# Weighted sum over experts on one core: VectorE's loop over single rounds, ScalarE copying the sums out

## The chip, the cores and the metric

The kernel runs on one core of a Trainium2 chip. The metric is the device time of one launch in microseconds (us). The kernel before took 704.42 us, the median of three runs (704.29 to 704.84).

## The reference

`expert_outputs` has the shape 16 x 1024 x 8 x 512 and `combine_weights` 16 x 1024 x 8, both float32. For each of the 16384 tokens the eight expert rows of 512 numbers are weighted and added:

```python
weights = combine_weights[..., np.newaxis]
return np.sum(expert_outputs * weights, axis=2).astype(np.float32)
```

268 MB are read and 33.6 MB written; each number read is used once.

## The kernel before

The 16384 tokens are 128 token rows of 128 partitions each, here called tiles; a tile is 128 x 8 x 512 numbers, 2 MB. The first 120 tiles are worked in 12 rounds of 10 tiles, the last 8 tiles are the tail.

One buffer, `ring`, holds the ten input tiles of a round. SyncE loads it in three chunks of 4, 4 and 2 tiles (L138); a chunk of the next round is loaded as soon as VectorE has finished the tiles of this round that stood there (the semaphore `done` counts finished tiles). The eight tail tiles are loaded the same way (L146), as one piece of three tiles and five of one.

VectorE does nearly all the arithmetic. For each chunk one instruction writes the product of expert 0 into `acc` (L227), and 14 instructions for each pair of tiles add the other seven experts (L217: `acc = ring * weight + acc`). `acc` holds 20 tiles, two halves of ten, and the loop body is two rounds (h = 0 and 1), run six times. The weights of a round are read from `w_c`, which ScalarE fills from `w_t` by one small copy a round (L173), after the store of two rounds before has landed, since that copy is also VectorE's leave to overwrite that half of `acc`.

ScalarE issues the stores of rounds 0 to 10 (L104), SyncE that of round 11. Round 8 (`SHARED`) is shared: ScalarE stores the middle half of each partition's row and GpSimd the two ends (L119, L122), with two tiny loads into `spare` around it (L127).

In the tail TensorE works as well. ScalarE scales an identity matrix by a column of weights (`diag`, L180, four buffers), and TensorE multiplies it with a tile's expert rows into PSUM (L193), 32 products in all, in the order of the tiles; a product needs its `diag` and its loaded tile. VectorE adds the remaining experts to what stands in PSUM (L217, L255), and one last addition (L269) closes tile 7. SyncE stores tiles 0 to 5 and then tiles 6 and 7 (L150).

All engines run in program order; what comes later in an engine's queue waits behind an instruction that waits.

Of the kernel before, what the change touches and what calls it, by code (L numbers as in the profile page):

```python
# [10 lines left out]
def kernel(  # L11
# [9 lines left out]

    nc = tc.nc
    fp32 = mybir.dt.float32
    mult, add = mybir.AluOpType.mult, mybir.AluOpType.add

    B, S, E, D = expert_outputs.shape
    T = B * S
    P = 128
    R = 10  # L40
    G = 2 * R
    T_P = T // P
    GROUPS = T_P // G
    LOOP = GROUPS * G
    TAIL = T_P - LOOP
    ROUNDS = LOOP // R
    CHUNKS = [(0, 4), (4, 4), (8, 2)]
    C = len(CHUNKS)
    DIAGS = 4
    OURS = 120  # L50
    END = 5 * D // 2
    APART = R * D - END
    SHARED = ROUNDS - 4

    x = expert_outputs.rearrange("b s e d -> (b s) e d")
    w = combine_weights.rearrange("b s e -> (b s) e")
    o = out.rearrange("b s d -> (b s) d")
    cut = LOOP * P
    x_g = x[0:cut].rearrange("(p n b g) e d -> n b p g e d", p=P, b=2, g=G)
    w_g = w[0:cut].rearrange("(p t) e -> p t e", p=P)  # L60
    o_g = o[0:cut].rearrange("(p n b g) d -> n b p g d", p=P, b=2, g=G)
    x_t = x[cut:T].rearrange("(p j) e d -> p j e d", j=TAIL)
    w_x = w[cut:T].rearrange("(p j) e -> p j e", j=TAIL)
    o_t = o[cut:T].rearrange("(p j) d -> p j d", j=TAIL)


    pe_e = [4, 4, 3, 3, 4, 5, 5, 4]
    tail_loads = [(0, 3)] + [(j, 1) for j in range(3, TAIL)]
# [4 lines left out]
    one = ctx.enter_context(tc.tile_pool(name="one", bufs=1))  # L73
    psum = ctx.enter_context(tc.tile_pool(name="psum", bufs=1, space=bass.MemoryType.PSUM))
    ring = one.tile([P, R, E, D], fp32, name="ring")
    acc = one.tile([P, G, D], fp32, name="acc")
    w_t = one.tile([P, T_P, E], fp32, name="w_t")
    w_c = one.tile([P, G, E], fp32, name="w_c")
    spare = one.tile([16, 8], fp32, name="spare")
    ident = one.tile([P, P], fp32, name="ident")  # L80
    diag = one.tile([P, DIAGS, P], fp32, name="diag")
    ps = psum.tile([P, TAIL, D], fp32, name="ps")

    sem = tc.alloc_semaphore
    w_in = sem("w_in")
    w_set = [sem(f"w_set{h}") for h in range(2)]
    loaded = [sem(f"loaded{c}") for c in range(C)]
    stored = [sem(f"stored{h}") for h in range(2)]
    rest_out = sem("rest_out")
    step = sem("step")  # L90
    done = sem("done")
    tail_in = [sem(f"tail_in{k}") for k in range(len(tail_loads))]
# [3 lines left out]
    product = sem("product")  # L96

    def store(queue, n):
        h = n % 2
        queue.wait_ge(done, (n + 1) * R)  # L100
        out = o_g[n // 4, n // 2 % 2].rearrange("p g d -> p (g d)")
        first, last = (END, APART) if n == SHARED else (h * R * D, (h + 1) * R * D)
        sums = acc.rearrange("p g d -> p (g d)")[:, first:last]
        queue.dma_start(out=out[:, first:last], in_=sums).then_inc(stored[h], 16)  # L104

    def ends(n, first, last):

        assert n % 2 == 0
        return [
            a.rearrange("p g d -> p (g d)")[:, 0 : 2 * APART]  # L110
            .rearrange("p (b k) -> p b k", b=2)[:, :, first:last]
            for a in (o_g[n // 4, n // 2 % 2], acc)
        ]

    def store_ends(gpsimd):
        turn(gpsimd, 4, 0)
        gpsimd.wait_ge(done, (SHARED + 1) * R)
        o_r, a_r = ends(SHARED, 0, END)
        gpsimd.dma_start(out=o_r[0:OURS], in_=a_r[0:OURS]).then_inc(rest_out, 16)  # L119
        for k in range(2):  # L120
            o_r, a_r = ends(SHARED, k * END // 2, (k + 1) * END // 2)
            gpsimd.dma_start(out=o_r[OURS:P], in_=a_r[OURS:P]).then_inc(rest_out, 16)  # L122
        turn(gpsimd, 13, 4)

    def turn(gpsimd, k, b):

        gpsimd.dma_start(  # L127
            out=spare[0:k, b : b + 4].rearrange("p (i j) -> p i j", i=2)[:, :, 0:1],
            in_=w[0 : 2 * k].rearrange("(p i) e -> p i e", i=2)[:, :, 0:1],
        ).then_inc(rest_out, 16)  # L130

    def loads_and_last_stores(sync):
        for n in range(ROUNDS):
            for c, (r, m) in enumerate(CHUNKS):
                if n:
                    sync.wait_ge(done, (n - 1) * R + r + m)
                g = n % 2 * R + r
                sync.dma_start(  # L138
                    out=ring[:, r : r + m], in_=x_g[n // 4, n // 2 % 2, :, g : g + m]
                ).then_inc(loaded[c], 16)  # L140
                if n == 0 and c == 0:
                    sync.dma_start(out=w_t[:, 0:LOOP], in_=w_g).then_inc(w_in, 16)
                    sync.dma_start(out=w_t[:, LOOP:T_P], in_=w_x).then_inc(w_in, 16)
        for k, (j, m) in enumerate(tail_loads):
            sync.wait_ge(done, LOOP - R + j + m)
            sync.dma_start(out=ring[:, j : j + m], in_=x_t[:, j : j + m]).then_inc(tail_in[k], 16)  # L146
        store(sync, ROUNDS - 1)
        for j, m in tail_stores:
            sync.wait_ge(done, LOOP + j + m)
            sync.dma_start(out=o_t[:, j : j + m], in_=acc[:, j : j + m]).then_inc(tail_out, 16)  # L150
# [12 lines left out]

    def weights_and_stores(scalar):
        scalar.wait_ge(w_in, 32)
        for n in range(ROUNDS):
            h = n % 2
            if n >= 2:
                store(scalar, n - 2)
                scalar.wait_ge(stored[h], 16 * (n // 2))  # L170
            if n == SHARED + 2:
                scalar.wait_ge(rest_out, 16 * 5)
            scalar.copy(  # L173
                out=w_c[:, h * R : h * R + R], in_=w_t[:, n * R : n * R + R]
            ).then_inc(w_set[h], 1)
        store(scalar, ROUNDS - 2)
        scalar.wait_ge(id_set, 2)
        scalar.wait_ge(stored[0], 16 * ROUNDS // 2)
        for k, (j, e) in enumerate(diags):
            i = scalar.mul(out=diag[:, k % DIAGS], in_=ident, mul=w_t[:, LOOP + j, e : e + 1])  # L180
            i.then_inc(diag_set, 1)
            if k >= DIAGS:
                i.wait_op(product, k - DIAGS + 1, "sem-ge")
        scalar.wait_ge(stored[1], 16 * ROUNDS // 2)

    def first_terms(tensor):
        for k, (j, e) in enumerate(diags):
# [13 lines left out]
    def terms(vector):  # L201
        def take(s, v):
            vector.wait_ge(s, v).then_inc(s, -v)  # L203

        last = {}

        def count(i, g, e):

            if e == E - 1:
                i.then_inc(done, 1)  # L210
            else:
                i.then_inc(step, 1)
                last["all"] = last.get("all", 0) + 1
                last[g] = last["all"]

        def fused(g, e, weight, before):
            return vector.scalar_tensor_tensor(  # L217
                out=acc[:, g], in0=ring[:, g % R, e], scalar=weight, in1=before, op0=mult, op1=add
            )

        with nc.Fori(0, GROUPS, engines=OrderedEngineSet([vector.engine])):
            for h in range(2):
                take(w_set[h], 1)
                for c, (r, m) in enumerate(CHUNKS):
                    take(loaded[c], 16)
                    q = h * R + r
                    i = vector.tensor_tensor(  # L227
                        out=acc[:, q : q + m],
                        in0=ring[:, r : r + m, 0],
                        in1=w_c[:, q : q + m, 0:1].to_broadcast([P, m, D]),  # L230
                        op=mult,
                    )
                    i.then_inc(step, 1)
                    last["all"] = last.get("all", 0) + 1
                    last.update((g, last["all"]) for g in range(q, q + m))
                    for g in range(q, q + m, 2):
                        for e in range(1, E):
                            for k in (g, g + 1):
                                i = fused(k, e, w_c[:, k, e : e + 1], acc[:, k])
                                i.wait_op(step, last[k], "sem-ge")  # L240
                                count(i, k, e)
            take(step, last["all"])

        last.clear()
# [1 line left out]
        def tail_term(j, e, end):  # L246
# [9 lines left out]
                i.wait_op(tail_in[-1], 16, "sem-ge")  # L256
            count(i, j, end)

        j = TAIL - 1
        for k in range(j - 1):  # L260
            for e in range(pe_e[k], E):
# [7 lines left out]
        i = vector.tensor_tensor(out=acc[:, j], in0=acc[:, j], in1=ps[:, j], op=add)  # L269
# [3 lines left out]
    with tc.tile_critical(no_gpsimd_drain=True):  # L273
        loads_and_last_stores(nc.sync)
        identity(nc.gpsimd)
        store_ends(nc.gpsimd)
        weights_and_stores(nc.scalar)
        first_terms(nc.tensor)
        terms(nc.vector)
# [35 lines left out]
```

## Time and profile before

| | before |
|---|---|
| median of the runs shown | 704.42 us |
| the profiled execution's own time | 704.37 us |
| its span, first to last instruction | 703.1 us |
| VectorE busy | 650.5 us (93%) |
| TensorE busy | 29.2 us (4%) |
| ScalarE busy | 16.8 us (2%) |
| moved by DMA over the span | 302.54 MB, mean 430 GB/s |

The 1.27 us between the profiled execution's time and its span lie outside the first and the last instruction. A digit in the rows of slices is the busy share of a fortieth of the span in tenths; 9 is 90% or more.

### The profile page before, as it was taken

To read this page: it belongs to the slowest core of one execution; us is meant where nothing else is said; L and a number is where in the kernel's file an instruction comes from. 1 tells how busy PE (TensorE), PEld (TensorE's weight loads), DVE (VectorE), ACT (ScalarE), POOL (GpSimd) and SP (SyncE) were. 2 spreads that over 40 slices of the span, in tenths; PEclk is the share of its full clock that TensorE was granted. 3 is DMA by queue.
4 is the path that set the end of the run, shared out by engine and by line. 5 is a ranking of instruction groups with operands and counts; after the bars stand their busy time and mean duration, and the time that the engine had idled before them with its cause. 6 is when DMAs were issued, how large, how long until landed. Compare 5 with 4: busy or idle time off the path is not lost. (4 is left out here: it accounts for less than half of the span.)

```text
span 703.1 us, 1288 instructions
## 1 busy us (share of the span) xinstructions
PE 29.2 (4%) x64; PEld 12.7 (2%) x64; DVE 650.5 (93%) x909; ACT 16.8 (2%) x45; POOL 3.9 (1%) x11
## 2 busy tenths in 40 slices
PE   0000000000000000000000000000000000000096
PEld 0000000000000000000000000000000000000042
DVE  0599999989989989989999998998999997999996
ACT  0000000000000000000000000000000000000042
POOL 0000000000000000000000000000010000000000
PEclk9999999999999999999999999999999999999999
DMA  9999999999999999999999999999999999999999
GB/s 414 392 474 418 399 436 447 416 439 431 440 424 475 404 431 447 428 416 439 429 437 454 440 400 465 418 448 417 421 458 403 466 421 448 429 415 422 432 430 391
DMA packets 8755, 302.54 MB, mean 430 GB/s; under 512 B 1200, under 2 KB 1200, under 8 KB 1712
## 3 DMA queue, kind: packets, MB, share of 16 engines
q1 hardware_dynamic: 6768, 273.68, 90.2%
q10 hardware_dynamic: 1584, 27.53, 9.1%
q0 software_dynamic: 400, 1.31, 0.5%
q14 instruction: 3, 0.02, 0.0%
HBM read 268.96 MB, written 33.55 MB: 430 GB/s over the span
## 5 line engine op out<-in xcount | busy, mean ns | idle before, releaser
L217 DVE SCALAR_TENSOR_TENSOR acc<-ring,w_c,acc 128x512 f32<-128x512 f32 x840 | 559.7, 745 | 1.3
L227 DVE TENSOR_TENSOR acc<-ring,w_c 128x2048 f32<-128x2048 f32 (+1 forms) x36 | 69.5, 1931 | 44.8 <-DVEq L203 44.8
L193 PE MATMUL ps<-ring,diag 128*128 128x512 f32 x64 | 29.2, 619 | 667.4 <-DMA ring<-in_expert_outputs_dram 667.4
L193 PEld LDWEIGHTS ps<-ring,diag 128*128 128x128 f32 x64 | 12.7, 201 | 683.0 <-DMA ring<-in_expert_outputs_dram 667.3
L217 DVE SCALAR_TENSOR_TENSOR acc<-ring,w_t,acc 128x512 f32<-128x512 f32 x24 | 17.7, 751 | 0.7
L173 ACT COPY w_c<-w_t 128x80 f32<-128x80 f32 x12 | 3.0, 257 | 585.8 <-DMA out_dram<-acc 484.3
L180 ACT ACTIVATE diag<-ident,w_t 128x128 f32<-128x128 f32 x32 | 12.5, 400 | 90.1 <-DMA out_dram<-acc 54.6
L217 DVE SCALAR_TENSOR_TENSOR acc<-ring,w_t,ps 128x512 f32<-128x512 f32 x7 | 5.2, 742 | 0.7 <-PE ps L193 0.7
L119 POOL DMA_DIRECT2D out_dram<-acc x1 | 0.8, 764 | 508.8 <-DVE acc L217 508.8
L173 ACT ACT_TABLE_LOAD x1 | 1.3, 1283 | 0.9 <-SPq L273 0.9
L127 POOL DMA_DIRECT2D spare<-in_combine_weights_dram x2 | 1.3, 645 | 0.3 <-issue 0.3
L122 POOL DMA_DIRECT2D out_dram<-acc x2 | 1.1, 564 | 0.0
L269 DVE TENSOR_TENSOR acc<-acc,ps 128x512 f32<-128x512 f32 x1 | 0.7, 686 | 0.1
L255 DVE TENSOR_SCALAR acc<-ring,w_t 128x512 f32<-128x512 f32 x1 | 0.5, 479 | 0.0
L154 POOL TENSOR_SCALAR_AFFINE_SELECT ident<-ident 128x128 f32<-128x128 f32 x1 | 0.3, 288 | 0.1
L153 POOL MEMSET ident<- 128x128 f32 x1 | 0.2, 205 | 0.5 <-SPq L273 0.5
L299 POOL MEMSET const-bfloat16-1.0<- 128x1 bf16 x1 | 0.1, 95 | 0.0
L299 POOL MEMSET const-uint8-127<- 128x1 uint8 x1 | 0.1, 95 | 0.0
L299 POOL MEMSET const-float32-0.0<- 128x1 f32 x1 | 0.1, 93 | 0.2 <-issue 0.2
L299 POOL MEMSET const-float32-1.0<- 128x1 f32 x1 | 0.1, 93 | 0.0
## 6 DMA issues: line engine op xcount, KB each, us to landing
ring<-in_expert_outputs_dram SPq DMA_DIRECT2D x12, 4096.0 KB, 34.0
out_dram<-acc ACTq DMA_DIRECT2D x10, 2560.0 KB, 26.7
ring<-in_expert_outputs_dram SPq DMA_DIRECT2D x5, 2048.0 KB, 28.6
ring<-in_expert_outputs_dram SPq DMA_DIRECT2D x1, 6144.0 KB, 27.6
out_dram<-acc SPq DMA_DIRECT2D x1, 2560.0 KB, 24.8
out_dram<-acc SPq DMA_DIRECT2D x1, 1536.0 KB, 9.7
out_dram<-acc ACTq DMA_DIRECT2D x1, 1280.0 KB, 24.5
out_dram<-acc POOLq DMA_DIRECT2D x1, 1200.0 KB, 36.8
```

The costliest lines, as they stand in the source:

```text
L119: gpsimd.dma_start(out=o_r[0:OURS], in_=a_r[0:OURS]).then_inc(rest_out, 16)
L122: gpsimd.dma_start(out=o_r[OURS:P], in_=a_r[OURS:P]).then_inc(rest_out, 16)
L127: gpsimd.dma_start(out=spare[0:k, b : b + 4].rearrange("p (i j) -> p i j", i=2)[:, :, 0:1], in_=w[0 : 2 * k].rearrange("(p i) e -> p i e", ...
L154: gpsimd.affine_select(out=ident, in_=ident, compare_op=mybir.AluOpType.not_equal, fill=1.0, base=0, pattern=[[-1, P]], channel_multiplier ...
L173: scalar.copy(out=w_c[:, h * R : h * R + R], in_=w_t[:, n * R : n * R + R]).then_inc(w_set[h], 1)
L180: i = scalar.mul(out=diag[:, k % DIAGS], in_=ident, mul=w_t[:, LOOP + j, e : e + 1])
L193: tensor.matmul(ps[:, j], lhsT=diag[:, k % DIAGS], rhs=ring[:, j, e], start=e == 0, stop=e == pe_e[j] - 1,).then_inc(product, 1)
L217: return vector.scalar_tensor_tensor(out=acc[:, g], in0=ring[:, g % R, e], scalar=weight, in1=before, op0=mult, op1=add)
L227: i = vector.tensor_tensor(out=acc[:, q : q + m], in0=ring[:, r : r + m, 0], in1=w_c[:, q : q + m, 0:1].to_broadcast([P, m, D]), op=mult,)
L255: i = vector.tensor_scalar_mul(out=acc[:, j], in0=x, scalar1=weight)
L269: i = vector.tensor_tensor(out=acc[:, j], in0=acc[:, j], in1=ps[:, j], op=add)
L299: nc = _bacc.Bacc("TRN2", target_bir_lowering=False, num_devices=1)
```

## The change

VectorE's loop body becomes one round, run twelve times; `acc` is ten tiles, and a second buffer of ten tiles, `sums`, is new. `head_slot` is an option of the loop: an instruction ahead of it (the row `ISA` below) sets where in the instruction memory the loop's first instruction stands. ScalarE copies each finished chunk from `acc` to `sums` (L125 of the new kernel), then copies that chunk's weights of the next round (L129), and after the third chunk stores `sums` (L84). Each chunk has a semaphore `ready` that tells VectorE it may start that chunk of the next round, `moved` counts the copied chunks, and `stored` the landed stores. The first copy of a round waits until the store of the round before has landed. GpSimd makes the identity matrix and issues no DMA. After the loop ScalarE makes the `diag` matrices as before; what it waited for ahead of the first (`stored[0]`) is gone. The round-11 store by SyncE waits for `moved`.

```diff
-    G = 2 * R
-    GROUPS = T_P // G
-    LOOP = GROUPS * G
+    ROUNDS = 12
+    LOOP = ROUNDS * R
...
-    acc = one.tile([P, G, D], fp32, name="acc")
+    acc = one.tile([P, R, D], fp32, name="acc")
+    sums = one.tile([P, R, D], fp32, name="sums")
...
+        queue.wait_ge(moved, (n + 1) * C)
+        queue.dma_start(out=o_r[n], in_=sums).then_inc(stored, 16)
...
-    def store_ends(gpsimd):
-        turn(gpsimd, 4, 0)
...
         scalar.wait_ge(w_in, 32)
+        for c, (r, m) in enumerate(CHUNKS):
+            scalar.copy(out=w_c[:, r : r + m], in_=w_t[:, r : r + m]).then_inc(ready[c], 1)
         for n in range(ROUNDS):
-            h = n % 2
-            if n >= 2:
-                store(scalar, n - 2)
-                scalar.wait_ge(stored[h], 16 * (n // 2))
-            if n == SHARED + 2:
-                scalar.wait_ge(rest_out, 16 * 5)
-            scalar.copy(
-                out=w_c[:, h * R : h * R + R], in_=w_t[:, n * R : n * R + R]
-            ).then_inc(w_set[h], 1)
-        store(scalar, ROUNDS - 2)
+            for c, (r, m) in enumerate(CHUNKS):
+                if n and c == 0:
+                    scalar.wait_ge(stored, 16 * n)
+                i = scalar.copy(out=sums[:, r : r + m], in_=acc[:, r : r + m])
+                i.wait_op(done, n * R + r + m, "sem-ge").then_inc(moved, 1)
+                if n + 1 < ROUNDS:
+                    t = (n + 1) * R + r
+                    i = scalar.copy(out=w_c[:, r : r + m], in_=w_t[:, t : t + m])
+                    i.wait_op(moved, n * C + c + 1, "sem-ge").then_inc(ready[c], 1)
+            if n + 1 < ROUNDS:
+                store(scalar, n)
         scalar.wait_ge(id_set, 2)
-        scalar.wait_ge(stored[0], 16 * ROUNDS // 2)
         for k, (j, e) in enumerate(diags):
...
-        with nc.Fori(0, GROUPS, engines=OrderedEngineSet([vector.engine])):
-            for h in range(2):
-                take(w_set[h], 1)
-                for c, (r, m) in enumerate(CHUNKS):
-                    take(loaded[c], 16)
...
+        with nc.Fori(
+            0, ROUNDS, engines=OrderedEngineSet([vector.engine]), head_slot={vector.engine: 128}
+        ):
+            for c, (r, m) in enumerate(CHUNKS):
+                take(ready[c], 1)
+                take(loaded[c], 16)
...
+        vector.wait_ge(moved, (ROUNDS - 1) * C + 2)
         j = TAIL - 1
```

On ScalarE, from the last small copies of the loop to its end, the kernel before has these instructions; `diag` are the matrices of the tail, and the names in brackets are the semaphores waited for.

```order
L173 COPY w_c<-w_t 128x80 [waits stored0]
L104 DMA out_dram<-acc 128x5120 [waits done]
L173 COPY w_c<-w_t 128x80 [waits stored1]
L104 DMA out_dram<-acc 128x5120 [waits done]
L180 ACTIVATE diag<-ident,w_t 128x128 [waits stored0,id_set]
L180 ACTIVATE diag<-ident,w_t 128x128 x3
L180 ACTIVATE diag<-ident,w_t 128x128 [waits product] x28
```

The changed kernel has these at the same place.

```order
L129 COPY w_c<-w_t 128x16 [waits moved]
L84 DMA out_dram<-sums 128x5120 [waits moved]
L125 COPY sums<-acc 128x2048 [waits stored,done]
L125 COPY sums<-acc 128x2048 [waits done]
L125 COPY sums<-acc 128x1024 [waits done]
L135 ACTIVATE diag<-ident,w_t 128x128 [waits id_set]
L135 ACTIVATE diag<-ident,w_t 128x128 x3
L135 ACTIVATE diag<-ident,w_t 128x128 [waits product] x28
```

The first `diag` stood behind the store of round 10 and its landing; now it stands behind the three copies of round 11, the last of which waits for the last tile of the loop.

On VectorE the loop body of the changed kernel is this, from the branch into it to the first instruction of the tail.

```order
L176 ISA
L176 UNCONDITIONAL_BRANCH
L182 TENSOR_TENSOR acc_62<-ring_61,w_c_65 128x2048 [waits ready0,loaded0]
L172 SCALAR_TENSOR_TENSOR acc_62<-ring_61,w_c_65,acc_62 128x512 [waits step] x28
L182 TENSOR_TENSOR acc_62<-ring_61,w_c_65 128x2048 [waits ready1,loaded1]
L172 SCALAR_TENSOR_TENSOR acc_62<-ring_61,w_c_65,acc_62 128x512 [waits step] x28
L182 TENSOR_TENSOR acc_62<-ring_61,w_c_65 128x1024 [waits ready2,loaded2]
L172 SCALAR_TENSOR_TENSOR acc_62<-ring_61,w_c_65,acc_62 128x512 [waits step] x14
L176 REGISTER_ALU [waits step]
L176 COMPARE_AND_BRANCH
L172 SCALAR_TENSOR_TENSOR acc_62<-ring_61,w_t_64,ps_68 128x512 [waits moved,product]
```

The arithmetic of a round is the same seventy-three instructions as in half of the body before; new are a wait for `ready` at each chunk and, at the tail, one for `moved`.

## Rows read from the trace of the kernel before

**Rows 1.** The page: the span and the DMA engines' busy share by slices.
```profile
span 703.1 us, 1288 instructions
DMA  9999999999999999999999999999999999999999
```

**Rows 2.** Stretches of the loop: engines' busy time, TensorE's clock, DMA share, GB/s.
```profile
24.70:129.40 104.70, 0.00 (x0) 0.00 (x0) 104.41 (x147) 0.26 (x1) 0.00 (x0) 1.00 1.01 435
129.40:619.40 490.00, 0.00 (x0) 0.00 (x0) 470.45 (x659) 2.32 (x9) 2.45 (x4) 1.00 1.00 433
```

**Rows 3.** Waits: who waited for whom, us in total, times, longest.
```profile
DVE acc L227 <- DVEq L203: 44.8, 11, 24.8
```

**Rows 4.** Timeline of VectorE: start, us, instructions, and the idle time before.
```profile
24.77 2.29 DVE L227 TENSOR_TENSOR acc<-ring,w_c 128x2048 f32<-128x2048 f32 x1 [24.77 <-DVEq L203]
...
77.07 2.28 DVE L227 TENSOR_TENSOR acc<-ring,w_c 128x2048 f32<-128x2048 f32 x1
...
120.08 9.37 DVE L217 SCALAR_TENSOR_TENSOR acc<-ring,w_c,acc 128x512 f32<-128x512 f32 x14
129.36 2.28 DVE L227 TENSOR_TENSOR acc<-ring,w_c 128x2048 f32<-128x2048 f32 x1
...
316.26 2.29 DVE L227 TENSOR_TENSOR acc<-ring,w_c 128x2048 f32<-128x2048 f32 x1 [2.05 <-DVEq L203]
```

**Rows 5.** Timeline of all engines from the first tail load to the loop's end.
```profile
639.67 23.34 SPq L146 DMA_DIRECT2D ring<-in_expert_outputs_dram  x6
641.68 2.29 DVE L227 TENSOR_TENSOR acc<-ring,w_c 128x2048 f32<-128x2048 f32 x1 [1.38 <-DVEq L203]
645.55 1.28 ACT L180 ACTIVATE diag<-ident,w_t 128x128 f32<-128x128 f32 x4 [54.59 <-DMA out_dram<-acc]
663.82 9.36 DVE L217 SCALAR_TENSOR_TENSOR acc<-ring,w_c,acc 128x512 f32<-128x512 f32 x14
667.35 0.50 PEld L193 LDWEIGHTS ps<-ring,diag 128*128 128x128 f32 x2 [667.35 <-DMA ring<-in_expert_outputs_dram]
667.38 29.20 PE L193 MATMUL ps<-ring,diag 128*128 128x512 f32 x64 [667.38 <-DMA ring<-in_expert_outputs_dram]
669.46 0.40 ACT L180 ACTIVATE diag<-ident,w_t 128x128 f32<-128x128 f32 x1 [22.63 <-PE ps L193]
670.07 0.34 PEld L193 LDWEIGHTS ps<-ring,diag 128*128 128x128 f32 x1 [0.52 <-ACT diag L180]
673.21 0.35 SPq L104 DMA_DIRECT2D out_dram<-acc  x1
```

**Rows 6.** The chain that ended last: start, us, what.
```profile
667.38 25.78 PE ps L193 x56
...
693.18 4.07 DVE acc L217 x6
...
697.35 0.69 DVE acc L269
```

**Rows 7.** Groups of instructions by line and shape: busy us, mean ns, idle before.
```profile
L217 DVE SCALAR_TENSOR_TENSOR acc<-ring,w_c,acc 128x512 f32<-128x512 f32 x840 | 559.7, 745 | 1.3
L227 DVE TENSOR_TENSOR acc<-ring,w_c 128x1024 f32<-128x1024 f32 x12 | 14.6, 1218 | 0.0
L217 DVE SCALAR_TENSOR_TENSOR acc<-ring,w_t,acc 128x512 f32<-128x512 f32 x24 | 17.7, 751 | 0.7
L173 ACT COPY w_c<-w_t 128x80 f32<-128x80 f32 x12 | 3.0, 257 | 585.8 <-DMA out_dram<-acc 484.3 <-DMA spare<-in_combine_weights_dram 79.4 <-DMA w_t<-in_combine_weights_dram 22.1
```

**Rows 8.** DMA issues: issuing engine, count, KB each, us from issue to landing.
```profile
out_dram<-acc ACTq DMA_DIRECT2D x10, 2560.0 KB, 26.7
out_dram<-acc SPq DMA_DIRECT2D x1, 1536.0 KB, 9.7
out_dram<-acc SPq DMA_DIRECT2D x1, 512.0 KB, 5.0
spare<-in_combine_weights_dram POOLq DMA_DIRECT2D x1, 0.1 KB, 49.6
```

More of the change, by code (lines that the diff above doesn't have):

```diff
@@ L40 @@
     R = 10
-    G = 2 * R
     T_P = T // P
-    GROUPS = T_P // G
-    LOOP = GROUPS * G
+    ROUNDS = 12
+    LOOP = ROUNDS * R
     TAIL = T_P - LOOP
-    ROUNDS = LOOP // R
     CHUNKS = [(0, 4), (4, 4), (8, 2)]
@@ L49 @@
     DIAGS = 4
[L50 to L53, printed above, removed]
     x = expert_outputs.rearrange("b s e d -> (b s) e d")
@@ L58 @@
     cut = LOOP * P
-    x_g = x[0:cut].rearrange("(p n b g) e d -> n b p g e d", p=P, b=2, g=G)
-    w_g = w[0:cut].rearrange("(p t) e -> p t e", p=P)
-    o_g = o[0:cut].rearrange("(p n b g) d -> n b p g d", p=P, b=2, g=G)
+    x_r = x[0:cut].rearrange("(p n g) e d -> n p g e d", p=P, g=R)
+    w_r = w[0:cut].rearrange("(p t) e -> p t e", p=P)
+    o_r = o[0:cut].rearrange("(p n g) d -> n p g d", p=P, g=R)
     x_t = x[cut:T].rearrange("(p j) e d -> p j e d", j=TAIL)
@@ L75 @@
     ring = one.tile([P, R, E, D], fp32, name="ring")
-    acc = one.tile([P, G, D], fp32, name="acc")
+    acc = one.tile([P, R, D], fp32, name="acc")
+    sums = one.tile([P, R, D], fp32, name="sums")
     w_t = one.tile([P, T_P, E], fp32, name="w_t")
-    w_c = one.tile([P, G, E], fp32, name="w_c")
-    spare = one.tile([16, 8], fp32, name="spare")
+    w_c = one.tile([P, R, E], fp32, name="w_c")
     ident = one.tile([P, P], fp32, name="ident")
@@ L85 @@
     w_in = sem("w_in")
-    w_set = [sem(f"w_set{h}") for h in range(2)]
+    ready = [sem(f"ready{c}") for c in range(C)]
     loaded = [sem(f"loaded{c}") for c in range(C)]
-    stored = [sem(f"stored{h}") for h in range(2)]
-    rest_out = sem("rest_out")
+    moved = sem("moved")
+    stored = sem("stored")
     step = sem("step")
@@ L98, in store @@
     def store(queue, n):
-        h = n % 2
[L100 to L113, printed above, removed]
-    def store_ends(gpsimd):
-        turn(gpsimd, 4, 0)
[L117 to L130, printed above, removed]
+        queue.wait_ge(moved, (n + 1) * C)
+        queue.dma_start(out=o_r[n], in_=sums).then_inc(stored, 16)
     def loads_and_last_stores(sync):
@@ L136, in loads_and_last_stores @@
                     sync.wait_ge(done, (n - 1) * R + r + m)
-                g = n % 2 * R + r
                 sync.dma_start(
-                    out=ring[:, r : r + m], in_=x_g[n // 4, n // 2 % 2, :, g : g + m]
+                    out=ring[:, r : r + m], in_=x_r[n, :, r : r + m]
                 ).then_inc(loaded[c], 16)
                 if n == 0 and c == 0:
-                    sync.dma_start(out=w_t[:, 0:LOOP], in_=w_g).then_inc(w_in, 16)
+                    sync.dma_start(out=w_t[:, 0:LOOP], in_=w_r).then_inc(w_in, 16)
                     sync.dma_start(out=w_t[:, LOOP:T_P], in_=w_x).then_inc(w_in, 16)
@@ L165, in weights_and_stores @@
         scalar.wait_ge(w_in, 32)
+        for c, (r, m) in enumerate(CHUNKS):
+            scalar.copy(out=w_c[:, r : r + m], in_=w_t[:, r : r + m]).then_inc(ready[c], 1)
         for n in range(ROUNDS):
-            h = n % 2
-            if n >= 2:
-                store(scalar, n - 2)
-                scalar.wait_ge(stored[h], 16 * (n // 2))
-            if n == SHARED + 2:
-                scalar.wait_ge(rest_out, 16 * 5)
-            scalar.copy(
-                out=w_c[:, h * R : h * R + R], in_=w_t[:, n * R : n * R + R]
-            ).then_inc(w_set[h], 1)
-        store(scalar, ROUNDS - 2)
+            for c, (r, m) in enumerate(CHUNKS):
[9 more added lines that the diff above has]
+                store(scalar, n)
         scalar.wait_ge(id_set, 2)
-        scalar.wait_ge(stored[0], 16 * ROUNDS // 2)
         for k, (j, e) in enumerate(diags):
@@ L183, in weights_and_stores @@
                 i.wait_op(product, k - DIAGS + 1, "sem-ge")
-        scalar.wait_ge(stored[1], 16 * ROUNDS // 2)
+        scalar.wait_ge(stored, 16 * ROUNDS)
     def first_terms(tensor):
@@ L217, in fused @@
             return vector.scalar_tensor_tensor(
-                out=acc[:, g], in0=ring[:, g % R, e], scalar=weight, in1=before, op0=mult, op1=add
+                out=acc[:, g], in0=ring[:, g, e], scalar=weight, in1=before, op0=mult, op1=add
             )
-        with nc.Fori(0, GROUPS, engines=OrderedEngineSet([vector.engine])):
-            for h in range(2):
-                take(w_set[h], 1)
-                for c, (r, m) in enumerate(CHUNKS):
-                    take(loaded[c], 16)
[L226 to L241, printed above, removed]
+        with nc.Fori(
[4 more added lines that the diff above has]
+                take(loaded[c], 16)
+                i = vector.tensor_tensor(
+                    out=acc[:, r : r + m],
+                    in0=ring[:, r : r + m, 0],
+                    in1=w_c[:, r : r + m, 0:1].to_broadcast([P, m, D]),
+                    op=mult,
+                )
+                i.then_inc(step, 1)
+                last["all"] = last.get("all", 0) + 1
+                last.update((g, last["all"]) for g in range(r, r + m))
+                for g in range(r, r + m, 2):
+                    for e in range(1, E):
+                        for k in (g, g + 1):
+                            i = fused(k, e, w_c[:, k, e : e + 1], acc[:, k])
+                            i.wait_op(step, last[k], "sem-ge")
+                            count(i, k, e)
             take(step, last["all"])
@@ L275 @@
         identity(nc.gpsimd)
-        store_ends(nc.gpsimd)
         weights_and_stores(nc.scalar)
```

## The prediction

> **What bounds the kernel now.** I read the page's slices first, then the stretches of the loop, then the waits, then VectorE's timeline, and last the end of the program in timeline and chain. The slices show the DMA engines at 90% or more in all forty [rows 1], and the two long stretches put their mean share at 1.00 to 1.01 with 433 to 435 GB/s [rows 2]. Nothing there is left over: a load can't come earlier unless another transfer goes away, and the change moves the same input and output.
>
> VectorE is a close second. Its first round runs without a wait from 24.77 to 77.07 [rows 4], so a round is 52.3 us of work. Its waits in the loop sum to 44.8 us, 24.8 of them the start [rows 3], so 20.0 are spread over the rounds. A typical one is 2.05 us ahead of a round's second chunk [rows 4], which makes a round 52.3 + 2.05 = 54.35 us. That is the cover: whatever slows VectorE by less than about 2 us a round is paid by a wait that stands there already.
>
> The end is different. The last chunk that VectorE waited for began at 641.68, and the loop ended at 663.82 + 9.36 = 673.18. Meanwhile ScalarE had made the first four diagonal matrices at 645.55, and TensorE was waiting only for its first tail tiles. It started at 667.38, 5.8 us before VectorE left the loop [rows 5]. From there the chain has no slack: 25.78 us of products, 4.07 us of VectorE's sums, one addition from 697.35 to 698.04 [rows 6], and a store of 512 KB that lands 5.0 us later [rows 8], at the span's end of 703.1. From TensorE's start to the last addition is 698.04 - 667.38 = 30.66 us.
>
> **The change, part by part.**
>
> *The diagonal matrices come later.* This is the term that I think decides. ScalarE runs in program order, and the first `diag` now stands behind the copy of the last chunk of round 11, which waits for the loop's last tile. The copy's start is 673.18 + 0.03 (the same signal reaches SyncE's store at 673.21 [rows 5]). Its length isn't in the trace. From below, ScalarE's copy of 80 numbers a partition takes 0.257 us; from above, that copy scaled to 1024 numbers is 3.3 us [rows 7]. VectorE's instruction on 128 x 1024 numbers, the nearest in size, takes 1.22 us [rows 7], and I take 1.2. Then one `diag` of 0.40 us, 0.21 us until TensorE loads it (669.46 + 0.40 to 670.07) and 0.03 us from that load to the product (667.35 to 667.38) [rows 5]. TensorE starts at 673.21 + 1.20 + 0.40 + 0.21 + 0.03 = 675.05 instead of 667.38, 7.67 us later.
>
> The Trainium skill (ScalarE: Activation LUTs, section "What ACT_TABLE_LOAD costs") gives an instruction with immediate scale and bias 186 ns + 0.833 ns per element of a partition. By that the copy would be an estimated 1.04 us and the sum 0.16 us lower; the 80-number copy agrees (0.25 against 0.257 us [rows 7]), but no run here shows the long one.
>
> TensorE's 29.2 us [rows 5] and its exchange with ScalarE don't change, and VectorE, which followed TensorE's lead in the tail, now waits between tiles, so the 30.66 us stay: the last addition ends at 705.71.
>
> *The last store.* It is issued 0.06 us after the addition and before took 5.0 us [rows 8], part of it behind the store of 1536 KB. That one was issued at about 692.1 and took 9.7 us, so until 701.8. By 705.7 it will have landed, and the last store meets empty queues. Its length there is at least 1.2 us (512 KB at 430 GB/s, the page's mean) and at most the 5.0 seen; between them I take the middle, 3.1. The span ends at 705.71 + 0.06 + 3.1 = 708.87. So 2 of the 7.7 us are given back by a queue that was busy before.
>
> *The wait of ScalarE's first copy for the store.* In round n it waits until the store of round n-1 has landed, and VectorE's first chunk of round n+1 waits for that copy and the small one behind it. Counted from the end E of round n-1: issue at about E + 1.5, landing after 26.7 us [rows 8] at E + 28.2, a copy of 2048 numbers (2 x 1.22) and a small one of 0.26 us [rows 7] end near E + 30.9. VectorE needs it at E + 54.35. There are 23 us to spare, so I take zero; beyond that each us of a late store is a us of VectorE's.
>
> *The copies beside VectorE.* ScalarE reads `acc` while VectorE works on other tiles. If they hinder each other, 2.05 us a round are covered. ScalarE's `diag` work beside VectorE in the tail didn't slow it (751 against 745 ns [rows 7]). I take zero.
>
> *Twelve back edges for six.* Between 120.08 + 9.37 and the next round's first instruction at 129.36, across a back edge of the old loop, there is no gap [rows 4]. Zero.
>
> *GpSimd's stores and tiny loads go,* and ScalarE's round-8 store becomes a full one: the same bytes on the same engines. The weights of a chunk come at their own signal; the first chunk's copy is shorter, worth some hundredths at 24.77. Stores start about 1.5 us later and so take a little less from the load of the next round's second chunk; and the order among the DMA engines' queues may shift. For this I allow the loop's end -1 to +1.5 us and put it at zero in the sum.
>
> *Sum.* 708.87 + 1.27 (the profiled execution's 704.37 less its span) = 710.14, and 0.05 for the median of 704.42 against the profiled 704.37: 710.2 us, 0.8% slower.
>
> **The rivals.**
>
> *Loads come earlier, and the end stays (not slower).* The place is VectorE's wait ahead of the second chunk. If a less crowded set of queues brought that chunk 0.65 us earlier in each round, the loop would end 12 x 0.65 = 7.7 us earlier, at 665.5, ScalarE's `diag` would be ready when the first tail tiles land at 667.3, and the program would end as before, 704. The 20 us of waits speak for it. Against it: the DMA share of 1.00 [rows 2]. If the DMA engines have no time free, neither that chunk nor the tail tiles can come earlier. It decides from about 6 us. Chance 0.07, of which 0.02 for a time under 703.
>
> *The copies hold VectorE (much slower).* If VectorE stood still through the three copies, about 2.4 + 2.4 + 1.2 = 6.0 us a round, less the 2.05 of cover, 12 rounds would add 47 us on top of the forecast: 757. With half of that stall it is 12 x 0.95 = 11 us: 721. It decides from 2.05 us a round; the tail's 751 ns speak against it. Chance 0.07.
>
> *The back edge stalls (slower).* If each of eleven back edges cost VectorE as much as a short store, 5.0 us [rows 8], less the cover, 11 x 2.95 = 32 us would come on top: 743. Small DMAs can be slow in the full queues: 49.6 us for one of GpSimd's [rows 8]. Against it stands the old loop's back edge without a gap. The Trainium skill (Runtime: NRT & Kernel Launch, section "Instruction fetch mechanics") says that a taken branch whose target lies outside the two pages held forces a fetch by DMA before execution goes on; by that rule a shorter body is the safer one, and the trace agrees so far as its longer body shows no such stop. Chance 0.03.
>
> **How the numbers follow.** The forecast keeps 0.83. Its own range: at the low end the loop ends 1 us earlier, the copy takes 0.26 and the store 1.2 us (710.2 - 1 - 0.95 - 1.9 = 706.4); at the high end 1.5 later, 3.3 and 5.0 (715.7). All at one end at once is unlikely; with about half of these, 707.8 to 712.9. It holds some 0.8 of everything, so I leave it as the range. A measurement of this kernel tells about 0.2%, 1.4 us, from no change; all of the forecast's range is above 705.8. Slower: 0.83 + 0.07 + 0.03 = 0.93; no change: 0.05; faster: 0.02.
>
> **What would show it.** In the profile after, TensorE's first product should start 1.5 to 2.5 us after the loop's last instruction, and its idle time should end on ScalarE's `diag`, not on a load. The wait named before ScalarE's first `diag` should be VectorE's. The loop's end should lie within 672 to 675. VectorE should now have some 5 to 8 us of waits on TensorE in the tail. The last store should land in about 3 us with the DMA share well under 1 in the last 8 us. The forecast is wrong if the loop ends before 668, or if VectorE's instructions of 745 ns have grown, or if waits for `ready` appear in the loop, or if a gap stands at each back edge.

## The result and the profile after

The changed kernel takes 710.51 us (median of four runs, 710.1 to 711.63) against 704.42 before; the ratio is 1.0088, with a 95% interval of 1.0073 to 1.0103. It is 0.9% slower, 0.3 us off the forecast of 710.2.

| | before | after |
|---|---|---|
| median | 704.42 us | 710.51 us |
| the profiled execution's own time | 704.37 us | 710.1 us |
| its span | 703.1 us | 708.7 us |
| VectorE busy | 650.5 us | 650.7 us |
| ScalarE busy | 16.8 us | 79.3 us |
| moved over the span | 430 GB/s | 427 GB/s |

The first thing to look for in the page after is where the DMA engines are no longer full. These are the row of the span and the row of slices, as in [rows 1].

```profile
span 708.7 us, 1396 instructions
DMA  9999999999999999999999999999999999999995
```

Thirty-nine slices are as full as before; the last one is half empty. The stretches of the loop tell the same: start and end, length, then busy time and count by engine (PE, weight loads, DVE, ACT, POOL), clock, DMA share and GB/s. The third stretch is the end of the program.

```profile
24.70:129.40 104.70, 0.00 (x0) 0.00 (x0) 103.79 (x146) 10.15 (x13) 0.00 (x0) 1.00 1.01 434
129.40:619.40 490.00, 0.00 (x0) 0.00 (x0) 470.96 (x658) 49.32 (x54) 0.00 (x0) 1.00 1.00 433
...
700.50:708.70 8.20, 4.12 (x10) 1.52 (x8) 4.75 (x7) 0.67 (x2) 0.00 (x0) 1.00 0.62 256
```

The loop moves its data at 433 to 434 GB/s as in [rows 2], and VectorE is as busy in the same stretches to within 0.6 us, though ScalarE now works beside it for about 10 us in each 100. Only the end has a share of 0.62. The kernel before also runs out of transfers at its end, but less:

```profile
696.50:703.10 6.60, 0.08 (x1) 0.00 (x0) 1.43 (x3) 0.00 (x0) 0.00 (x0) 0.85 0.77 322
```

VectorE's long instructions are no slower beside the copies; this is their group in the changed kernel (busy us, mean ns, idle before), to be held against [rows 7].

```profile
L172 DVE SCALAR_TENSOR_TENSOR acc<-ring,w_c,acc 128x512 f32<-128x512 f32 x840 | 559.7, 745 | 1.3
```

The waits of the changed kernel (who waited for whom, us in total, times, longest) name what ends it.

```profile
PE ps L148 <- ACT diag L135: 675.5, 1, 675.5
...
ACT sums L125 <- DMA out_dram<-sums: 279.7, 11, 25.8
DVE acc L182 <- DVEq L158: 45.5, 11, 25.4
...
DVE acc L172 <- PE ps L148: 7.8, 3, 6.7
```

TensorE's one long wait ends on ScalarE's `diag`; in [rows 5] it ended on a load. VectorE's waits in the loop are 45.5 - 25.4 = 20.1 us beside the start, against 44.8 - 24.8 = 20.0 in [rows 3], so the chunks' waits for `ready` and for their loads together are no longer than the waits before. In the tail VectorE now waits 7.8 us for TensorE.

The end in order of time is in the timeline (start, us, engine, line, instruction, count, idle time before and its releaser).

```profile
664.57 9.36 DVE L172 SCALAR_TENSOR_TENSOR acc<-ring,w_c,acc 128x512 f32<-128x512 f32 x14
673.97 1.04 ACT L125 COPY sums<-acc 128x1024 f32<-128x1024 f32 x1 [8.63 <-DVE acc L172]
674.92 1.27 ACT L135 ACTIVATE diag<-ident,w_t 128x128 f32<-128x128 f32 x4
...
675.43 0.50 PEld L148 LDWEIGHTS ps<-ring,diag 128*128 128x128 f32 x2 [675.43 <-issue]
675.46 1.19 PE L148 MATMUL ps<-ring,diag 128*128 128x512 f32 x1 [675.46 <-ACT diag L135]
```

The chain that ended last (start, us, what) now runs from the loop straight through ScalarE.

```profile
673.97 1.04 ACT sums L125
675.01 0.31 ACT diag L135
675.32 0.14 issue
675.46 25.74 PE ps L148 x56
...
701.23 4.07 DVE acc L172 x6
...
705.39 0.69 DVE acc L225
```

In [rows 6] the same 25.78 + 4.07 + 0.69 us stood behind a load, at 667.38. They are moved by 8.08 us (675.46 against 667.38), and the last addition ends at 706.08 instead of 698.04. The DMA issues (count, KB, median us from issue to landing) show what is given back.

```profile
out_dram<-sums ACTq DMA_DIRECT2D x11, 2560.0 KB, 25.6
...
out_dram<-sums SPq DMA_DIRECT2D x1, 2560.0 KB, 23.5
out_dram<-acc SPq DMA_DIRECT2D x1, 1536.0 KB, 5.1
out_dram<-acc SPq DMA_DIRECT2D x1, 512.0 KB, 2.6
```

SyncE's row for the last two stores starts with the issue of the first of them, first in the kernel before, then in the changed one.

```profile
692.12 6.27 SPq L150 DMA_DIRECT2D out_dram<-acc  x2
```

```profile
700.07 6.37 SPq L103 DMA_DIRECT2D out_dram<-acc  x2
```

The store of 1536 KB is issued at 700.07 and lands at about 705.2, before the last store is issued behind the addition's end at 706.08. In the kernel before it landed at 701.8, after the last store's issue. With nothing ahead of it, the last store lands 2.6 us after its issue, not 5.0 as in [rows 8]. So 8.0 us later at the last addition is 5.6 us more of span.

### The profile page after: what moved, and what is told of

It is laid out like the page before. It is cut to its first block, busy times and chain, and to the rows that moved or that the text cites. A ratio compares the mean times of both kernels' runs of the same rounds, so it can differ in the third digit from the quotient of the medians.

```text
span 708.7 us, 1396 instructions
## 1 busy us (share of the span) xinstructions
PE 29.2 (4%) x64; PEld 12.7 (2%) x64; DVE 650.7 (92%) x909; ACT 79.3 (11%) x105; POOL 0.7 (0%) x6
## 5 line engine op out<-in xcount | busy, mean ns | idle before, releaser
L125 ACT COPY sums<-acc 128x2048 f32<-128x2048 f32 (+1 forms) x36 | 58.1, 1614 | 583.5 <-DVE acc L172 303.8
L182 DVE TENSOR_TENSOR acc<-ring,w_c 128x2048 f32<-128x2048 f32 (+1 forms) x36 | 69.5, 1930 | 45.5 <-DVEq L158 45.5
L129 ACT COPY w_c<-w_t 128x32 f32<-128x32 f32 (+1 forms) x33 | 7.0, 213 | 1.1
L120 ACT COPY w_c<-w_t 128x32 f32<-128x32 f32 (+1 forms) x3 | 0.4, 210 | 22.7 <-DMA w_t<-in_combine_weights_dram 22.7
## 6 DMA issues: line engine op xcount, KB each, us to landing
out_dram<-sums SPq DMA_DIRECT2D x1, 2560.0 KB, 23.5
```

Source lines behind the costliest of these rows:

```text
L120: scalar.copy(out=w_c[:, r : r + m], in_=w_t[:, r : r + m]).then_inc(ready[c], 1)
L125: i = scalar.copy(out=sums[:, r : r + m], in_=acc[:, r : r + m])
L129: i = scalar.copy(out=w_c[:, r : r + m], in_=w_t[:, t : t + m])
L182: i = vector.tensor_tensor(out=acc[:, r : r + m], in0=ring[:, r : r + m, 0], in1=w_c[:, r : r + m, 0:1].to_broadcast([P, m, D]), op=mult,)
```

## The experiments

All times are medians, beside runs of the kernel before on the same chip (704.48 us for experiments 1, 2, 4 and 7, 704.46 us for 3, 5, 6 and 8). The rows stand in the order of the experiments.

| | time | ratio to the kernel before |
|---|---|---|
| last chunk stored straight from `acc` | 704.89 | 1.0006 (0.9997 to 1.0015) |
| kernel before, `diag` after the loop | 709.68 | 1.0073 (1.0058 to 1.0088) |
| four more copies | 713.41 | 1.0125 (1.0110 to 1.0141) |
| four `diag` ahead of the last copy | 705.29 | 1.0012 (1.0003 to 1.0021) |
| changed kernel without `head_slot` | 710.44 | 1.0090 (1.0074 to 1.0105) |
| first experiment without `head_slot` | 704.71 | 1.0005 (0.9996 to 1.0014) |
| kernel before without GpSimd's share | 705.60 | 1.0018 (1.0009 to 1.0027) |
| first experiment with half a share | 705.07 | 1.0010 (1.0001 to 1.0019) |

**1. Take the last copy out of ScalarE's way.** Tiles 8 and 9 of round 11 are never overwritten in the tail, so they need no copy.

```diff
-        store(sync, ROUNDS - 1)
+        sync.wait_ge(moved, n * C + C - 1)
+        sync.dma_start(out=o_r[n, :, 0:r], in_=sums[:, 0:r]).then_inc(stored, 16)
+        sync.wait_ge(done, LOOP)
+        sync.dma_start(out=o_r[n, :, r : r + m], in_=acc[:, r : r + m]).then_inc(stored, 16)
...
+                if (n, c) == (ROUNDS - 1, C - 1):
+                    break
                 i = scalar.copy(out=sums[:, r : r + m], in_=acc[:, r : r + m])
```

> The changed kernel, but the last chunk of round 11 (tiles 8 and 9, which the tail never overwrites) is stored straight from acc, so ScalarE's diagonal matrices stand behind the copy of the second chunk only, which is done about 2 us before the first tail tiles land. Theory (the late diagonal matrices are the whole loss): TensorE starts at about 667.9 on its load again, VectorE leaves the loop at about 673.9 as in the changed kernel, and the time is 704.3 to 705.2 us. Rival (the loss comes from the rest of the change: one acc buffer, the waits for ready, twelve back edges, no share for GpSimd): TensorE starts at 667.9 as well, but the time stays above 708.5 us.

704.89 us: 5.6 us of the 6.1 come back. The other parts of the change are in place, with one thing moved besides: the round-11 store goes out in two pieces, its first 2048 KB at 665.21 and not with the rest at 675.03. The chain of this kernel:

```profile
639.60 28.28 DMA ring<-in_expert_outputs_dram
667.88 0.09 issue
667.97 26.49 PE ps L154 x56
```

TensorE waits for its load again, so the tail hangs on the DMA engines as in the kernel before. The single `acc` buffer, the waits for `ready`, the copies and the twelve back edges together cost at most what the interval leaves, 0.15%. That is a net figure: TensorE starts 0.59 us later than in [rows 6] and its 56 instructions take 0.71 us longer, but from the last addition to the span's end it is 4.0 us (699.34 to 703.3) instead of 5.1 (698.04 to 703.1). Experiment 4 leaves the round-11 store as the change has it.

**2. Put the late `diag` alone into the kernel before.**

```diff
         scalar.wait_ge(stored[0], 16 * ROUNDS // 2)
+        scalar.wait_ge(done, LOOP)
         for k, (j, e) in enumerate(diags):
```

> The kernel before with one wait more: ScalarE makes the first diagonal matrix only after the last tile of the loop. Nothing else of the change is in it. Theory: TensorE starts about 0.5 us after the loop's end at 673.2, so at 673.7 instead of 667.4, the last addition ends near 704.3, the last store takes 2.6 us on empty queues, and the time is 708.2 us (707.5 to 709). Rival (the store queues had room enough to hide a late tail, and the loss comes from the other parts): not above 705.5 us.

709.68 us, 5.2 us slower: one wait makes most of the loss. The rival is refuted. The time is above my 708.2 and its bounds, and the chain shows by what:

```profile
673.34 0.41 ACT diag L181
673.75 0.14 issue
673.89 27.18 PE ps L194 x56
```

TensorE started at 673.89, near the 673.7 expected, but its 56 instructions took 27.18 us, not the 25.78 of [rows 6]. The weight loads show it. First those of this kernel, then those of the changed one (start, us, idle time before):

```profile
678.29 0.34 PEld L194 LDWEIGHTS ps<-ring,diag 128*128 128x128 f32 x1 [0.52 <-ACT diag L181]
679.14 0.34 PEld L194 LDWEIGHTS ps<-ring,diag 128*128 128x128 f32 x1 [0.52 <-issue]
679.86 0.19 PEld L194 LDWEIGHTS ps<-ring,diag 128*128 128x128 f32 x1 [0.38 <-issue]
680.29 0.19 PEld L194 LDWEIGHTS ps<-ring,diag 128*128 128x128 f32 x1 [0.24 <-issue]
```

```profile
677.30 0.33 PEld L148 LDWEIGHTS ps<-ring,diag 128*128 128x128 f32 x1 [0.52 <-issue]
678.15 0.32 PEld L148 LDWEIGHTS ps<-ring,diag 128*128 128x128 f32 x1 [0.52 <-ACT diag L135]
678.71 0.19 PEld L148 LDWEIGHTS ps<-ring,diag 128*128 128x128 f32 x1 [0.24 <-issue]
679.14 0.19 PEld L148 LDWEIGHTS ps<-ring,diag 128*128 128x128 f32 x1 [0.24 <-issue]
```

TensorE begins at half its pace, a load every 0.85 us, and goes over to one every 0.43 us: here 6.0 us after its start (673.89 to 679.86), in the changed kernel 3.3 us after (675.46 to 678.71), which is also the kernel before's figure (667.35 to 670.66). That step is 1.4 us of the excess; the excess is 1.5 us for the median and 1.9 us for the profiled execution, which was the longest of the four.

**3. More delay at the same place.** Four copies of 128 x 512 numbers into the not yet used `diag` buffers stand ahead of the first `diag`.

```diff
         scalar.wait_ge(id_set, 2)
+        for k in range(4):
+            i = scalar.copy(out=diag.rearrange("p k c -> p (k c)"), in_=acc[:, R - 1])
+            if k:
+                i.wait_op(more, k, "sem-ge")
+            i.then_inc(more, 1)
+        scalar.wait_ge(more, 4)
```

> The changed kernel with four more ScalarE copies of 128 x 512 numbers, one waiting for the other, between the last copy and the first diagonal matrix; they change no output. Theory (from the last copy on, TensorE, VectorE and the last store form one chain without slack): each copy is about 0.61 us (the measured 1.04 us for 1024 and 1.90 us for 2048 numbers) and a few hundredths for its wait, 2.6 us together, and the time rises by as much, to 713.1 us (712.5 to 713.8). Rival (part of a late start is still absorbed in the tail): a rise of under 1.3 us.

713.41 us, 2.9 us more. In the profiled execution (714.14 us) the chain has the copies at 0.63 us and TensorE 2.55 us later than in the changed kernel, again with a long slow start (27.23 us for the 56):

```profile
676.81 0.63 ACT diag L136
677.44 0.02 issue
677.46 0.41 ACT diag L142
677.87 0.14 issue
678.01 27.23 PE ps L155 x56
```

That execution is 4.0 us longer than the changed kernel's profiled one (710.1): the 2.55 us of delay and 1.49 us of slow start. The four runs lie in two pairs, 712.6 to 712.7 and 714.1 to 714.5, so the 2.9 us between the medians owe something to chance. Even the shortest run is 2.5 us above the changed kernel's shortest, so the delay is paid in full and the rival, a rise of under 1.3 us, is out.

**4. Only the first four `diag` early.**

```diff
+                if (n, c) == (ROUNDS - 1, C - 1):
+                    scalar.wait_ge(id_set, 2)
+                    make_diags(scalar, 0, DIAGS)
                 i = scalar.copy(out=sums[:, r : r + m], in_=acc[:, r : r + m])
...
+        make_diags(scalar, DIAGS, len(diags))
```

> The changed kernel with the first four diagonal matrices made ahead of the last copy; the other 28 stay behind it. Theory: TensorE starts at 667.9, makes four products until about 673.2 (the first ones at the slow clock), stops until about 675.4 for the fifth matrix, and ends near 699.5 if its clock stays up, 701.4 if it falls in the stop: 704.9 or 706.7 us. Rival (only the loop's end or the rest of the change counts): as the changed kernel, 710.5 us.

705.29 us, near the 704.9 of the case in which TensorE keeps its pace. The last copy and the round-11 store stand here as in the changed kernel, and 5.2 us of the 6.1 come back by the order of ScalarE's queue alone. Its timeline shows the early products, the stop, and the rest:

```profile
668.58 6.05 PE L153 MATMUL ps<-ring,diag 128*128 128x512 f32 x8 [668.58 <-DMA ring<-in_expert_outputs_dram]
675.91 24.27 PE L153 MATMUL ps<-ring,diag 128*128 128x512 f32 x56 [1.28 <-ACT diag L119]
```

The 56 instructions behind the stop of 1.28 us (the last 28 of the 32 products, two instructions each) take 24.27 us, 0.43 each, the full pace from the first on. The slow start was spent ahead of the stop.

**5. and 6. The place of the loop in the instruction memory.** The option is taken out of the changed kernel, and of the first experiment.

```diff
-        with nc.Fori(
-            0, ROUNDS, engines=OrderedEngineSet([vector.engine]), head_slot={vector.engine: 128}
-        ):
+        with nc.Fori(0, ROUNDS, engines=OrderedEngineSet([vector.engine])):
```

> The changed kernel without head_slot: the loop's first instruction stands where it falls. Theory (a back edge costs VectorE nothing in either place): 710.5 us (709.8 to 711.5), no gap at the back edges. Rival (a body that lies across two blocks is fetched again at each back edge): gaps of 1 us and more ahead of a round's first instruction and a time above 712 us.

> The first experiment (last chunk stored straight from acc) without head_slot. There the DMA engines end the program again, so a DMA effect of where the loop stands could show. Theory: 704.9 us as with head_slot (704.3 to 705.4), since the fetch of instructions is a few packets of some KB either way. Rival (a fetch of instructions in the middle of the loop delays one DMA engine, and that engine ends the program): 705.4 to 706.5 us, like the kernel before without its share.

710.44 and 704.71 us: no difference from 710.51 and 704.89 that can be measured. The end of the second round and the start of the third in the changed kernel without the option, over its back edge:

```profile
120.09 9.37 DVE L172 SCALAR_TENSOR_TENSOR acc<-ring,w_c,acc 128x512 f32<-128x512 f32 x14
129.37 2.29 DVE L180 TENSOR_TENSOR acc<-ring,w_c 128x2048 f32<-128x2048 f32 x1
```

No gap stands there, as in [rows 4] and in the changed kernel (120.69 + 9.36, next round at 129.97).

**7. GpSimd's share alone.** The kernel before without it: `store` always takes the whole half, `store_ends` and the wait for `rest_out` are gone.

```diff
-        first, last = (END, APART) if n == SHARED else (h * R * D, (h + 1) * R * D)
+        first, last = h * R * D, (h + 1) * R * D
...
-            if n == SHARED + 2:
-                scalar.wait_ge(rest_out, 16 * 5)
...
-        store_ends(nc.gpsimd)
```

> The kernel before without GpSimd's part: ScalarE stores round 8 whole, the tiny loads into spare and the wait for them are gone. Theory of the prediction (same bytes on the same engines, nothing gained or lost): 703.7 to 705.2 us. Rival (the share evened out the sixteen DMA engines: in the kernel before VectorE's wait of 2.05 us ahead of a round's second chunk is gone in the round after the shared store): the wait stays in that round, some engine ends later, and the time is 705.5 to 707.5 us.

705.60 us, 1.1 us slower (0.6 to 1.9 by the interval). The prediction put this part at nothing; the rival is right as to its size, and its sign in the trace is there too. First the kernel before, in the round after the shared store, then this kernel in the same round:

```profile
531.83 2.28 DVE L227 TENSOR_TENSOR acc<-ring,w_c 128x2048 f32<-128x2048 f32 x1
```

```profile
533.40 2.29 DVE L225 TENSOR_TENSOR acc<-ring,w_c 128x2048 f32<-128x2048 f32 x1 [2.06 <-DVEq L201]
```

The wait of 2.06 us stays without the share. What it is worth to the loop shows in VectorE's starts on the second chunks of rounds 8 and 11, the last before GpSimd's stores and the last of the loop. The kernel before has 479.53 and, in [rows 5], 641.68, so 162.15 us; this kernel needs 163.30:

```profile
479.53 2.29 DVE L227 TENSOR_TENSOR acc<-ring,w_c 128x2048 f32<-128x2048 f32 x1 [2.04 <-DVEq L203]
```

```profile
478.96 2.29 DVE L225 TENSOR_TENSOR acc<-ring,w_c 128x2048 f32<-128x2048 f32 x1 [2.05 <-DVEq L201]
...
642.26 2.29 DVE L225 TENSOR_TENSOR acc<-ring,w_c 128x2048 f32<-128x2048 f32 x1 [2.05 <-DVEq L201]
```

The same stretch takes 162.48 us in experiment 2, which has the full share, and 163.26 to 163.30 us in all seven traces without a share. So the full share brings the loop's end 0.8 to 1.1 us forward. The time itself is made up otherwise: up to round 8 this kernel is 0.57 us ahead, so its tail tiles land only 0.57 us later, and TensorE's 56 instructions take 0.76 us longer by their slow start; 0.2 us come back at the last store (4.8 us instead of 5.0).

```profile
667.95 26.54 PE ps L191 x56
```

Whether that slow start comes with the missing share or with the execution is not shown, nor that one DMA engine lags and is relieved by the share.

**8. A share for the first experiment.** GpSimd stores the first 1280 numbers of each partition of round 8 from `sums`, in pieces as before, with the tiny loads around them.

```diff
-        queue.dma_start(out=o_r[n], in_=sums).then_inc(stored, 16)
+        first = 2 * END if n == SHARED else 0
+        queue.dma_start(
+            out=o_r[n].rearrange("p g d -> p (g d)")[:, first:],
+            in_=sums.rearrange("p g d -> p (g d)")[:, first:],
+        ).then_inc(stored, 16)
...
+        store_part(nc.gpsimd)
```

> The first experiment with a share for GpSimd as in the kernel before, half as large: of round 8 it stores the first 1280 numbers a partition from sums, with the tiny loads around it. Theory (the share is worth about 1 us by evening out the DMA engines, as its removal from the kernel before showed): 704.0 to 704.5 us. Rival (with the shorter loop body no engine is behind, so the share has nothing to even out): 704.7 to 705.2 us.

705.07 us against 704.89 without: the rival is right, the half share gains nothing here, and its stretch from round 8 to round 11 takes 163.46 us, as without a share. By what the full share shortens that stretch stays open. The half share differs in more than its size, since it is stored from `sums`, behind ScalarE's copies. No version beat the kernel before; the best of the changed kind, 704.71 us, can't be told from it.

## Why the prediction was right, point by point

*The bound.* The DMA engines stayed full to the last slice, and VectorE's waits of about 2 us a round stood where they had been, as forecast, but for the round after GpSimd's stores (below). The rival of earlier loads needed a gap in the DMA share, and there was none.

*The late `diag`.* This is nearly the whole case: experiment 1 takes it out and 5.6 us come back, 4 takes out its first four and 5.2 us come back, 2 puts it alone into the kernel before and 5.2 us appear, 3 lengthens it and the time follows. The step from loop to TensorE came out by its terms so:

| term | forecast | measured |
|---|---|---|
| loop's end | 673.18 | 664.57 + 9.36 = 673.93 |
| last tile to copy | 0.03 | 0.04 |
| copy of 128 x 1024 | 1.20 | 1.04 |
| first `diag` | 0.40 | 0.31 |
| `diag` to TensorE's product | 0.24 | 0.14 |
| TensorE starts | 675.05 | 675.46 |
| from there to the last addition's end | 30.66 | 30.62 |
| last store, issue to landing | 3.1 | 2.6 |
| span | 708.87 | 708.7 |

The chain counts the first `diag` from the copy's end; it began 0.09 us before that (674.92 against 675.01). The copy was the term for which the nearest row was VectorE's 1.22 us. The Trainium skill (ScalarE: Activation LUTs, section "What ACT_TABLE_LOAD costs") made it an estimated 1.04 us. The trace agrees, with 1.04 us (and 1.90 us for 2048 numbers).

*The loop's end* was put at zero in the sum with an allowance of -1 to +1.5; it came 0.75 us later. The mis-sized step is "the same bytes on the same engines". VectorE's starts on the second chunks of rounds 8 and 11 in the changed kernel show where the time went:

```profile
479.17 2.29 DVE L182 TENSOR_TENSOR acc<-ring,w_c 128x2048 f32<-128x2048 f32 x1 [2.05 <-DVEq L158]
...
642.43 2.29 DVE L182 TENSOR_TENSOR acc<-ring,w_c 128x2048 f32<-128x2048 f32 x1 [2.03 <-DVEq L158]
```

At round 8 it is 0.36 us ahead of the kernel before (479.53), at round 11 it is 0.75 us behind (641.68). The 1.11 us between match the 1.15 us that experiment 7 loses over the same rounds, and the 0.75 us go straight into the chain.

*Luck in the sum.* Its errors nearly cancelled: +0.75, then -0.34 on the way to TensorE, and -0.5 on the last store. The 30.66 us from TensorE's start held because its slow start lasted 3.3 us in both profiled executions; in experiments 2 and 3 it lasted 6.0 us, and the same stretch was 1.4 us longer. The prediction had no term for that. Nor do two small slips of sums matter: 12 x 0.65 is 7.8 and not 7.7, and half of the low end's errors would give 708.3 and not 707.8.

*The wait for the store* was as sized: its longest was 25.8 us, and VectorE never waited for it. *The copies beside VectorE* did nothing: its instructions take 745 ns as in [rows 7], with ScalarE busy 79.3 us instead of 16.8. *The back edges* have no gap in the rows of the three kernels looked at. So both slower rivals fell.

*The store queues as a partial cover:* of 8.0 us at the last addition 5.6 reached the span. The forecast had it as 7.67 against 5.8, but by a step that failed. It left the store of 1536 KB at its old issue, about 692.1, so that it had landed at 701.8. That store waits for VectorE's sums and moved with the tail, to 700.07; with its old 9.7 us it would have landed at 709.8, behind the last store. It took 5.1 us instead. Before its issue SyncE's round-11 store of 2560 KB had landed (675.03 + 23.5 = 698.5), while in the kernel before that store, issued at 673.21 and 24.8 us on the way, landed at 698.0, almost 6 us after the issue at 692.12. So the queues were free for a reason that the prediction did not have.

## What to carry to other kernels

When an engine gets new work, look at what stands behind it in that engine's program order, above all where the work of another stage begins: 1.04 us of copying cost more than 5 us because it waited for the loop's last tile with TensorE's first weights queued behind it. A buffer that will not be overwritten again needs no copy, and the last pass of a loop is where this holds. And in a program that is bound by its transfers, check which engine becomes the last one at the end before counting the middle: a tail that starts late takes the end over. When a tail is moved in a sum, everything that waits for it moves too, its stores included.

## What the runs showed of the hardware

TensorE's slow start is not a constant to add. In experiment 2 the granted clock reads 1.00, the level of 2.4 GHz, in every stretch of 4 us from 664 to 684, yet after its long idle time TensorE first runs at half its pace: 6 matmul instructions in the stretch 676 to 680, 11 in the next. In the profiled executions it goes over to the full pace in 3.3 us (the kernel before and the changed kernel) to 6.0 us (experiments 2 and 3); the 56 instructions took 25.74 to 27.23 us accordingly. There is one profiled execution for each kernel, so whether the program or the execution decides is not shown. With a stop of 1.28 us behind its slow start, in experiment 4, it went on at the full pace.

With `head_slot` VectorE's first instruction came at 25.4 us, without it at 24.8, where the prediction had it. Nothing came of it: the loop ends at 673.93 with it and at 673.86 without.

A store of 2.5 MB of which GpSimd takes half in uneven pieces shortened the stretch from round 8 to round 11 from 163.30 to 162.15 us, in a loop whose DMA share is 1.00; a quarter taken from another buffer did not (163.46).
